# Row sums in 64 columns, spread factors by token halves, and three moved casts in a two-layer hybrid block

## The chip, the cores and the metric

The kernel runs on one core of a Trainium2 chip. The metric is device time in microseconds (us) of one execution; lower is better. Three timed runs of the kernel before gave 1850.76 us in the median (1850.59 to 1853.43).

## What is computed

The reference is a two-layer transformer block for one sequence of 256 tokens plus 256 context tokens, width 2048, everything in float32:

```
for layer i in (0, 1):
    shift, scale, gate = split(silu(c) @ ada_w[i] + ada_b[i])         # for x; the same with c_ctx for the context
    h  = rmsnorm(x,  norm_g[i]) * (1 + scale)   + shift
    hc = rmsnorm(xc, norm_g[i]) * (1 + scale_c) + shift_c
    layer 0: u, z = split(h @ w_in);  f = real(fft2(u by 16 groups of 256)) mixed by w_mix;  y = f * silu(z)   (x and xc)
    layer 1: q, k, v, z = split(h @ w_in);  rope on q and k;  attention with a sink over a window of 128 and the context;  y = o * silu(z)   (x alone)
    x  = x  + gate   * (y  @ w_out[i])
    xc = xc + gate_c * (yc @ w_out[i])                                # layer 0 alone
return rmsnorm(x, final_g)
```

`rmsnorm` divides each token's row by the root of its mean square. Layer 1 therefore needs, for each of 512 tokens, a sum over all 2048 features of layer 0's result before it can begin.

## The kernel before, in words

**Number format.** Products run on TensorE (PE) in a reduced float32 format. Each operand is split into a high part `h` (a cast, L61, on ScalarE, ACT) and a low part `l = x - h` (L62, on VectorE, DVE), and each product is three matmuls: h·h, h·l, l·h (`mm3`, L74 to L76). `half_split` (L64) splits one half (1024 columns) of a 1 MB weight tile from the pool `raw` into two tiles of the pool `ws` (6 tiles, so three pairs).

**Stages.** Stage 1 (0 to about 150 us) normalises x, makes its Fourier transform over tokens (`dft`, L238), makes layer 0's scale and shift from 32 loads of 1 MB (`ada`, L271; its matmuls are L276, four to a load), and makes the first six 128-row blocks of the gate `z` (`z_load`, `z_w`, `z_x`, `z_step`, L299 to L338). The 16 steps `k` over the features come in four rounds of four (`for i in range(4)`, L418): a round needs the scale and shift of its own features, so four `ada` loads with `which` = 1 and four with `which` = 0 for round i+1 stand among the steps of round i, with the two gate weight tiles of round i+1 (`wa` for four blocks, `wb` for two). All of these loads go through SyncE's queue (SP) in one order, into five 1 MB buffers: three of the pool `raw`, two of `raw2` (`raw_st`, L173). A load can be issued only when the instruction that last read its buffer is done: four `ada` matmuls on PE, or the splits of a gate weight tile on DVE.

Stage 2 (to about 450 us) goes through 16 Fourier groups, stage 3 makes the rest of the gate, and stage 4 (to 1018.5 us) multiplies with `w_out` of layer 0. Each of its 16 feature blocks leaves PSUM through `evac0` (L702), which also squares it (L710, ACT) and adds the squares up in `sqs[0]` (L714, L720) or leaves them in `sqs[1]`.

**The boundary of the layers** is what the change mostly touches. `x1_turn` (L758) transposes four blocks of layer 0's result into one PSUM bank (four matmuls against the identity, L761), copies it out on ACT (L763) and sends it to DRAM (L764), for two halves of the tokens and four column blocks `c`, eight times in all; `turns` (L766) queues such a pair behind named instructions. The kernel before does `c` = 0 and 1, then the row sums, then `c` = 2 and 3. A row sum (L790) is a matmul with a matrix of ones as the stationary operand and 256 columns of squares as the moving one, so every one of 128 partitions gets the sums of 256 tokens. `root` (L81) makes 1/sqrt of it on that whole 128x256 tile: a square root on ACT (L82), then on DVE a scaled copy (L83), a reciprocal (L86) and three more operations (L87 to L89). It runs twice, for x and for the context. Then, per feature block `k`, `ht` = x · scale · factor (L827, DVE), its shifted high part (L828, ACT) and its low part (L829, DVE) make the operands `hx` and `hc` of the key and value product: 16 steps of 24 matmuls on 8 PSUM banks (L74 to L76, in the loop that begins at L835). [...]

**The first keys.** After that product the keys are rotated and transposed (L866, L868), and `prep_kk` (L902) casts each key head twice into `kkh` (L908, ACT) and makes `kkl` (L910, GpSimd, POOL). The heads 0 and 1 are prepared while the query product begins.

**What sets the order.** A scheduler in the framework orders each engine's instructions when the program is built, from a model of their times; `tc.issue_after(i)` keeps instructions of a block behind `i` on `i`'s engine. The order on each engine is then fixed. Pools hand out buffers, and the reader of a buffer must be done before its next load.

Of the kernel before, what the change touches and what calls it, by code (L numbers as in the profile page):

```python
# [16 lines left out]
P = 128  # L17
# [12 lines left out]
def tile_dit(ctx: ExitStack, tc: tile.TileContext, a: dict, out: bass.AP):  # L30
# [33 lines left out]
    def half_split(t, i):  # L64
        h = wsp.tile([P, 1024], F32R, tag="ws", name="wh")
        l = wsp.tile([P, 1024], F32R, tag="ws", name="wl")
        split(h, l, t[:, i * 1024 : (i + 1) * 1024])
        return h, l

    def ws_split(t):  # L70
# [93 lines left out]
    with tc.tile_pool(name="st", reuse_waits="tile", bufs=1, side="right") as st, ExitStack() as sts:  # L164
# [22 lines left out]
        def ext(dt=F32):  # L187
            return extp[0].tile([P, 512], dt, tag="ext", name="ext")
# [115 lines left out]
        def z_w(i, wa, wb):  # L304
            pa = [half_split(wa, j) for j in range(2)]
            pb = []
            for b in range(NE - 4):
                h, l = ext(F32R), ext(F32R)
                split(h, l, wb[:, b * 512 : (b + 1) * 512])
                pb.append((h, l))  # L310
            for j in range(4):
                zw[4 * i + j] = [
                    *(tuple(t[:, (j % 2) * 512 + b * P : (j % 2) * 512 + (b + 1) * P] for t in pa[j // 2]) for b in range(4)),
                    *(tuple(t[:, j * P : (j + 1) * P] for t in p) for p in pb),
                ]
# [4 lines left out]
        def z_x(k):  # L320
            h, l = ext(F32R), ext(F32R)
            for s in range(2):
# [84 lines left out]
        ada(1, 1, 1)  # L407
        wr = z_load(0)
        dft(1, 2)
        dft(1, 3)  # L410
        sta.close()
# [4 lines left out]
        cl = ub.tile([P, 4, P], F32R, name="cl")  # L416
        z_w(0, *wr)
        for i in range(4):  # L418
            k = 4 * i
            for j in range(4):  # L420
                z_x(k + j)
            hx_prep(k)
# [335 lines left out]
    def x1_turn(tb, c):  # L758
        o = psum()
        for j in range(4):  # L760
            p_end[0] = PE.transpose(o[:, j * P : (j + 1) * P], x1[c * 4 + j][:, tb * P : (tb + 1) * P], ident).ins  # L761
        t = act()
        S.copy(t, o)  # L763
        nc.scalar.dma_start(x1d[tb, :, c * 512 : (c + 1) * 512], t)  # L764

    def turns(c, *after):  # L766
        with ExitStack() as es:
            for i in after:
                es.enter_context(tc.issue_after(i))
            for tb in range(2):  # L770
                x1_turn(tb, c)

    p_end = [None]
    o = psum()
# [5 lines left out]
    for c in range(2):  # L780
        turns(c, sq_end[0], p_end[0])
    with tc.issue_after(add_end[0]):
        V.tensor_tensor(kv_l, kv_raw[:, 0:1024], kv_h.bitcast(F32), op=ALU.subtract)
    r_bc1, qv, qt = act(), act(), act()
    for s in range(2):
        q = slice(s * N, (s + 1) * N)
        o = psum()[:, 0:N]
        with tc.issue_after(p_end[0]):
            for i in (1, 0):
                last = PE.matmul(o, ones[:, 0:1].broadcast_to([P, P]), sqs[i][:, q], start=i == 1, stop=i == 0).ins  # L790
        p_end[0] = last
        rooted = root(r_bc1[:, q], qv[:, q], qt[:, q], o)[0]
    for c in range(2, 4):
        turns(c, p_end[0], rooted)
    lay0.close()
# [19 lines left out]
    with tc.tile_pool(name="h1", reuse_waits="tile", bufs=16) as h1p:  # L815
# [3 lines left out]
        with tc.tile_pool(name="kvp", reuse_waits="tile", bufs=2) as kvp:  # L819
            hc1 = []  # L820
            for k in range(KT):
# [3 lines left out]
                for s, h in ((0, hx), (1, hc)):  # L825
                    q = slice(s * N, (s + 1) * N)
                    V.scalar_tensor_tensor(t[:, q], x1[k][:, q], gs1[:, k, s : s + 1], r_bc1[:, q], op0=ALU.mult, op1=ALU.mult)  # L827
                    S.activation(h[:, 0:N], t[:, q], AF.Identity, bias=sh1[:, k, s : s + 1])  # L828
                    hx_end = V.scalar_tensor_tensor(h[:, N : 2 * N], t[:, q], sh1[:, k, s : s + 1], h[:, 0:N].bitcast(F32), op0=ALU.add, op1=ALU.subtract).ins  # L829
                if k == 0:  # L830
                    hx_first = hx_end
                hx1.append(hx)
                hc1.append(hc)
            o = [[psum() for _ in range(2)] for _ in range(4)]
            for kg in range(8):  # L835
                w = [(kv_h, kv_l)] if kg == 0 else ws_split(raw(a["wkv"][kg]))
                for j in range(2):
                    k = kg * 2 + j
                    if k == 1:
                        with tc.issue_after(hx_first):  # L840
                            w.append(half_split(kv_raw, 1))
# [33 lines left out]
        with tc.tile_pool(name="at", reuse_waits="tile", bufs=2) as at:  # L875

            kk, qq, obs, szs = {}, {}, {}, {}
            defer = []
# [16 lines left out]
            def o1_step(k, os_, wh, wl):  # L895
                while len(yh) <= min(k + 2, NB - 1) and (len(yh) < 20 or fin):
                    y_split(len(yh))
# [4 lines left out]
            def prep_kk(hk):  # L902
                kkh = at.tile([P, 512], F32R, tag="kkh", name="kkh")
                kkl = at.tile([P, 512], F32R, tag="kkl", name="kkl")
                b = (hk % 2) * 64
                src = kT[hk // 2][b : b + 64, :]
                for c in (0, 64):
                    S.copy(kkh[c : c + 64, :], src)  # L908
                for c in (0, 64):
                    GP.tensor_tensor(kkl[c : c + 64, :], src, kkh[b : b + 64, :].bitcast(F32), op=ALU.subtract)  # L910
                kk[hk] = (kkh, kkl)
# [66 lines left out]
            def emit_unit():  # L978
# [5 lines left out]
                if pos[0] + 1 < len(ulist):  # L984
                    ready[pos[0] + 1] = prep(ulist[pos[0] + 1])
                w = ready.pop(pos[0])
                pos[0] += 1
                kind, n, i, o = u
# [349 lines left out]
```

## Time and profile before

| what | value |
|---|---|
| median of three timed runs | 1850.76 us |
| the profiled execution's own time | 1852.08 us |
| its span, first to last instruction | 1850.3 us |
| matmuls busy (PE) | 1817.7 us, 98% |
| DVE, ACT, POOL busy | 1418.7, 984.6, 154.6 us |
| DMA, mean over the span | 196 GB/s |
| DMA between 94 and 101 us | 428 GB/s |
| granted TensorE clock, 1030 to 1036 us | 0.50 |
| granted TensorE clock over the span, mean | 0.997 |

The profiled execution took 1852.08 us, of which 1850.3 us lie between its first and last instruction. PE is the busiest engine by far, so what counts is where PE stands still: the view of waits says who ended each such wait, and the view of the chain of waits follows the end of the kernel back through them. A window gives the busy time of each engine, the clock granted to TensorE (1.00 is full) and the share and rate of DMA in one stretch. In the timeline each row has a start, a length, the engine, the line, the operation, output<-inputs, and in brackets the idle time ahead of it.

### The profile page before, as it was taken

The page shows a single profiled execution, that of the slowest core. Times are in us where ns is not written, and L with a number is a line of the kernel's source. Part 1 is how long each engine was busy: PE and PEld are TensorE (multiplying, and loading weights), DVE is VectorE, ACT ScalarE, POOL GpSimd, SP SyncE. Part 2 cuts the span into 40 slices and gives each one's busy share as a digit, 9 for nine tenths or more (in the row PEclk, how much of TensorE's full clock was granted, in tenths as well). Part 3 has the DMA queues.
Part 4 walks back from the last instruction along what each step waited for, and adds up shares of the span by engine and source line. Part 5 has one row for each costly group of instructions (what it writes and reads, how often), then busy time and mean ns, then how long its engine had stood idle before and what let it go on. Part 6 is the DMA issues. An engine that isn't in the chain of part 4 may idle for free.

```text
span 1850.3 us, 26316 instructions
## 1 busy us (share of the span) xinstructions
PE 1817.7 (98%) x9933; PEld 1550.2 (84%) x9933; DVE 1418.7 (77%) x2429; ACT 984.6 (53%) x1733; POOL 154.6 (8%) x178
## 2 busy tenths in 40 slices
PE   8999999999999999999999899999999999999998
PEld 6669999988888888888888787888888888887886
DVE  5668999969788897579964926878878878887455
ACT  6545444543322242314322514888888888897343
POOL 0001000010000000000000001121220220300001
PEclk9999999999999999999999999999999999999999
DMA  9985665476676667664674333333333333434553
GB/s 364 336 337 196 214 208 188 168 267 261 259 278 252 238 220 268 238 231 153 231 280 168 115 110 140 121 131 137 115 121 131 137 117 134 160 137 175 189 182 137
DMA packets 64223, 362.75 MB, mean 196 GB/s; under 512 B 7776, under 2 KB 7920, under 8 KB 30048
## 3 DMA queue, kind: packets, MB, share of 16 engines
q1 hardware_dynamic: 52592, 326.41, 48.7%
q0 software_dynamic: 7472, 27.71, 3.9%
q10 hardware_dynamic: 4032, 6.95, 1.1%
q8 instruction: 78, 1.28, 0.3%
q14 instruction: 49, 0.40, 0.1%
HBM read 346.87 MB, written 14.16 MB: 195 GB/s over the span
## 4 chain that ended last, share of the span: by engine, by line
PE 93%; DVE 2%; ACT 2%; DMA 1%; issue 1%; POOL 0%; SPq 0%; ACTq 0%; DVEq 0%; POOLq 0%
PE ps L74 24%; PE ps L75 24%; PE ps L76 24%; PE ps L1014 6%; PE ps L1016 3%; PE ps L1070 3%; PE ps L1085 2%; PE ps L1084 2%; PE ps L1050 2%; PE ps L1051 2%; PE ps L276 1%; DVE wl L62 1%; DMA raw<-in_awp 0%; ACT wh L61 0%; DMA act<-in_xT 0%
## 5 line engine op out<-in xcount | busy, mean ns | idle before, releaser
L61 ACT CAST wh<-raw 128x1024 fp32r<-128x1024 f32 x328 | 344.1, 1053 | 449.0 <-PE ps L75 326.2
L62 DVE TENSOR_TENSOR wl<-raw,wh 128x1024 fp32r<-128x1024 f32 x328 | 414.5, 1267 | 201.2 <-ACT wh L61 198.5
L75 PE MATMUL ps<-act,wh 128*128 128x512 f32 x928 | 361.1, 389 | 0.0
L74 PE MATMUL ps<-act,wh 128*128 128x512 f32 x928 | 357.6, 389 | 0.0
L76 PE MATMUL ps<-act,wl 128*128 128x512 f32 x928 | 356.3, 389 | 0.0
L75 PEld LDWEIGHTS ps<-act,wh 128*128 128x128 f32 x928 | 174.2, 188 | 36.4 <-DVE act L641 0.2
L76 PEld LDWEIGHTS ps<-act,wl 128*128 128x128 f32 x928 | 174.2, 188 | 36.3 <-DVE wl L62 0.2
L74 PEld LDWEIGHTS ps<-act,wh 128*128 128x128 f32 x928 | 174.1, 188 | 36.2 <-ACT act L640 0.3
L1014 PE MATMUL ps<-h,wh 128*128 128x512 f32 x512 | 186.8, 400 | 0.0
L611 DVE CUSTOM_DVE_ANT_0 raw<-raw,cb 128x1024 f32<-128x1024 f32 x128 | 155.0, 1221 | 35.1 <-DMA raw<-in_adw 34.1
L611 DVE CUSTOM_DVE_ANT_0 junk<-raw,cb 128x1024 f32<-128x1024 f32 x96 | 117.2, 1221 | 32.7 <-DMA raw<-in_adw 19.0
L1016 PE MATMUL ps<-h,wl 128*128 128x256 f32 x512 | 138.1, 280 | 0.0
L74 PE MATMUL ps<-wh,h 128*128 128x512 f32 x320 | 125.1, 399 | 6.3 <-ACT h L828 6.3
L75 PE MATMUL ps<-wl,h 128*128 128x512 f32 x320 | 126.5, 395 | 1.5 <-DVE wl L62 1.5
L76 PE MATMUL ps<-wh,h 128*128 128x512 f32 x320 | 124.4, 391 | 0.0
L1014 PEld LDWEIGHTS ps<-h,wh 128*128 128x128 f32 x512 | 96.1, 188 | 18.7
L1052 DVE CUSTOM_DVE_ANT_0 ps<-ps,mask,nsink 128x512 f32<-128x512 f32 x128 | 92.1, 754 | 11.8 <-PE ps L1051 10.6
L1055 ACT ACTIVATE p<-ps,mx 128x512 f32<-128x512 f32 x128 | 87.3, 687 | 24.6 <-DVE mx L1052 24.0
L1016 PEld LDWEIGHTS ps<-h,wl 128*128 128x128 f32 x512 | 96.8, 189 | 1.4
L62 DVE TENSOR_TENSOR pl<-ps,ph 128x512 fp32r<-128x512 f32 x128 | 83.7, 685 | 10.0 <-ACT ph L61 8.9
L1060 ACT ACTIVATE p<-p,sm 128x512 f32<-128x512 f32 x128 | 85.5, 718 | 7.8 <-DVE sm L1058 7.8
L75 PE MATMUL ps<-wl,ys 128*128 128x512 f32 (+1 forms) x216 | 84.0, 389 | 0.0
(328 smaller groups left out, 3790.5 us busy)
## 6 DMA issues: line engine op xcount, KB each, us to landing
raw<-in_adw SPq DMA_DIRECT2D x64, 1024.0 KB, 5.3
raw<-in_wz SPq DMA_DIRECT2D x62, 1024.0 KB, 4.9
raw<-in_awp SPq DMA_DIRECT2D x32, 1024.0 KB, 7.8
raw<-in_wo SPq DMA_DIRECT2D x32, 1024.0 KB, 5.7
raw<-in_wq SPq DMA_DIRECT2D x32, 1024.0 KB, 4.8
raw<-in_wu SPq DMA_DIRECT2D x25, 1016.0 KB, 5.5
raw<-in_wo1b SPq DMA_DIRECT2D x16, 1024.0 KB, 4.8
act<-in_xT POOLq DMA_DIRECT2D x32, 256.0 KB, 5.8
```

The source lines that it names most:

```text
L61: S.copy(h, src)
L62: V.tensor_tensor(l, src, h.bitcast(F32), op=ALU.subtract)
L74: PE.matmul(o, wh, xh, start=start, stop=False)
L75: PE.matmul(o, wh, xl, start=False, stop=False)
L76: PE.matmul(o, wl, xh, start=False, stop=stop)
L611: V.tensor_tensor_reduce(junk if s == 0 and i < 3 else wf, wf, cb[:, s], 1.0, 0.0, ALU.mult, ALU.add, acc[:, i, kh, fg * 2 + f, s : s + 1])
L1014: PE.matmul(o[0], wh[:, q], hx1[k], start=k == 0, stop=k == KT - 1)
L1016: PE.matmul(o[0][:, 0:N], wl[:, q], hx1[k][:, 0:N], start=False, stop=False)
L1052: V.tensor_tensor_reduce(o, o, mask[:, tb, :], -0.125, nsink[:, i : i + 1], ALU.add, ALU.min, mx[:, tb : tb + 1])
L1055: S.activation(pt[:, tb, :], so[tb], AF.Exp, bias=mx[:, tb : tb + 1], scale=-1.0, accum_out=sm[:, tb : tb + 1])
L1060: S.activation(pt[:, tb, :], pt[:, tb, :], AF.Copy, scale=sm[:, tb : tb + 1])
L1070: PE.transpose(o[:, (kt * 2 + tb) * P : (kt * 2 + tb + 1) * P], pt[:, tb, c : c + P], ident)
```

## The change

In stage 1, `half_split` keeps its last cast in `cast[0]`. The gate weights of round 0 are split (`z_w(0)`) ahead of the last two transforms, with `wb` split as one half into `ws` tiles in place of four `ext` tiles, and the operand of step 0 (`z_x(0)`) is made ahead of the last transform, in `act` tiles.

At the boundary, the turns of `c` = 0 and 1 only transpose at first; `x1_out` copies and sends later. The row sums use the squares as the stationary operand and 64 columns of ones as the moving one, four token blocks in turn, so that a sum lies on its token's partition. `root` runs once, on one column of each block (128x4). The turns of `c` = 2 follow, then two matmuls for each token half spread the factors over all partitions (as `bcast_rows` does, L98), ACT copies each half out, and the first `ht` (k = 0) reads it from PSUM. The turns of `c` = 3 follow; four of the eight copies out wait for the first shifted high parts (`hx_act`).

In the attention stage, the casts of the keys 0 and 1 wait for the weight cast of the fourth unit (`kk_hold`); `kkl` of head 0 is made on DVE. In the last product, layer 1's results are split up to six steps ahead (two before) while `k` < 12.

```diff
--- before
+++ after
@@ -64,8 +64,11 @@
     def half_split(t, i):
         h = wsp.tile([P, 1024], F32R, tag="ws", name="wh")
         l = wsp.tile([P, 1024], F32R, tag="ws", name="wl")
-        split(h, l, t[:, i * 1024 : (i + 1) * 1024])
+        cast[0] = S.copy(h, t[:, i * 1024 : (i + 1) * 1024]).ins
+        V.tensor_tensor(l, t[:, i * 1024 : (i + 1) * 1024], h.bitcast(F32), op=ALU.subtract)
         return h, l
+
+    cast = [None]
 
     def ws_split(t):
         return [half_split(t, i) for i in range(2)]
@@ -305,8 +308,13 @@
             pa = [half_split(wa, j) for j in range(2)]
             pb = []
             for b in range(NE - 4):
-                h, l = ext(F32R), ext(F32R)
-                split(h, l, wb[:, b * 512 : (b + 1) * 512])
+                if i == 0:
+                    if b == 0:
+                        h0, l0 = half_split(wb, 0)
+                    h, l = (t[:, b * 512 : (b + 1) * 512] for t in (h0, l0))
+                else:
+                    h, l = ext(F32R), ext(F32R)
+                    split(h, l, wb[:, b * 512 : (b + 1) * 512])
                 pb.append((h, l))
             for j in range(4):
                 zw[4 * i + j] = [
@@ -318,7 +326,7 @@
         z_l = {}
 
         def z_x(k):
-            h, l = ext(F32R), ext(F32R)
+            h, l = (ext(F32R), ext(F32R)) if k else (act(F32R), act(F32R))
             for s in range(2):
                 q = slice(s * N, (s + 1) * N)
                 t = xT[k // 2][s][:, (k % 2) * N : (k % 2 + 1) * N]
@@ -405,8 +413,9 @@
         turn(0, 0, rows)
         ada(1, 1, 0)
         ada(1, 1, 1)
-        wr = z_load(0)
+        z_w(0, *z_load(0))
         dft(1, 2)
+        z_x(0)
         dft(1, 3)
         sta.close()
         wfp = us.enter_context(tc.tile_pool(name="wfp", reuse_waits="tile", bufs=8))
@@ -414,11 +423,11 @@
         ub = us.enter_context(tc.tile_pool(name="ub", reuse_waits="tile", bufs=1))
         ch = ub.tile([P, 4, P], F32R, name="ch")
         cl = ub.tile([P, 4, P], F32R, name="cl")
-        z_w(0, *wr)
         for i in range(4):
             k = 4 * i
             for j in range(4):
-                z_x(k + j)
+                if k + j:
+                    z_x(k + j)
             hx_prep(k)
             if 0 < i < 3:
                 ada(i + 1, 1, 0)
@@ -759,18 +768,14 @@
         o = psum()
         for j in range(4):
             p_end[0] = PE.transpose(o[:, j * P : (j + 1) * P], x1[c * 4 + j][:, tb * P : (tb + 1) * P], ident).ins
+        turned.append((tb, c, o))
+
+    def x1_out(tb, c, o):
         t = act()
         S.copy(t, o)
         nc.scalar.dma_start(x1d[tb, :, c * 512 : (c + 1) * 512], t)
 
-    def turns(c, *after):
-        with ExitStack() as es:
-            for i in after:
-                es.enter_context(tc.issue_after(i))
-            for tb in range(2):
-                x1_turn(tb, c)
-
-    p_end = [None]
+    p_end, turned = [None], []
     o = psum()
     p_end[0] = PE.transpose(o[0:KT, 0:P], gt1.rearrange("p k s -> p (k s)"), ident).ins
     gr = const.tile([KT, P], F32, name="gr")
@@ -778,20 +783,40 @@
         S.copy(gr, o[0:KT, 0:P])
     nc.gpsimd.dma_start(gated.rearrange("o (k p) -> (o k) p", p=P), gr)
     for c in range(2):
-        turns(c, sq_end[0], p_end[0])
+        with tc.issue_after(p_end[0]):
+            for tb in range(2):
+                x1_turn(tb, c)
+    with tc.issue_after(sq_end[0]):
+        for _ in range(2):
+            x1_out(*turned.pop(0))
+    o = psum()
+    for i in (1, 0):
+        for t in range(4):
+            with tc.issue_after(p_end[0]):
+                p_end[0] = PE.matmul(o[:, t * 64 : (t + 1) * 64], sqs[i][:, t * P : (t + 1) * P], ones[:, 0:1].broadcast_to([P, 64]), start=i == 1 and t == 0, stop=i == 0 and t == 3).ins
+    qr, qv, qt = (const.tile([P, 4], F32, name=f"q{n}") for n in "rvt")
     with tc.issue_after(add_end[0]):
-        V.tensor_tensor(kv_l, kv_raw[:, 0:1024], kv_h.bitcast(F32), op=ALU.subtract)
-    r_bc1, qv, qt = act(), act(), act()
+        add_end[0] = V.tensor_tensor(kv_l, kv_raw[:, 0:1024], kv_h.bitcast(F32), op=ALU.subtract).ins
+    with tc.issue_after(add_end[0]):
+        rooted, q_end = root(qr, qv, qt, o.rearrange("p (t c) -> p t c", c=64)[:, 0:4, 0])
+    with tc.issue_after(rooted):
+        for _ in range(2):
+            x1_out(*turned.pop(0))
+    with tc.issue_after(p_end[0]):
+        for tb in range(2):
+            x1_turn(tb, 2)
+    r_bc1 = act()
+    rows1 = []
     for s in range(2):
-        q = slice(s * N, (s + 1) * N)
         o = psum()[:, 0:N]
-        with tc.issue_after(p_end[0]):
-            for i in (1, 0):
-                last = PE.matmul(o, ones[:, 0:1].broadcast_to([P, P]), sqs[i][:, q], start=i == 1, stop=i == 0).ins
-        p_end[0] = last
-        rooted = root(r_bc1[:, q], qv[:, q], qt[:, q], o)[0]
-    for c in range(2, 4):
-        turns(c, p_end[0], rooted)
+        for t in range(2):
+            with tc.issue_after(p_end[0]):
+                p_end[0] = PE.matmul(o[:, t * P : (t + 1) * P], qr[:, 2 * s + t : 2 * s + t + 1].broadcast_to([P, P]), ident, start=True, stop=True).ins
+        spread = S.copy(r_bc1[:, s * N : (s + 1) * N], o).ins
+        rows1.append(o)
+    with tc.issue_after(p_end[0]):
+        for tb in range(2):
+            x1_turn(tb, 3)
     lay0.close()
 
     l1c = ctx.enter_context(tc.tile_pool(name="l1c", reuse_waits="tile", bufs=1))
@@ -824,11 +849,14 @@
                 t = kvp.tile([P, 512], F32, tag="ht", name="ht")
                 for s, h in ((0, hx), (1, hc)):
                     q = slice(s * N, (s + 1) * N)
-                    V.scalar_tensor_tensor(t[:, q], x1[k][:, q], gs1[:, k, s : s + 1], r_bc1[:, q], op0=ALU.mult, op1=ALU.mult)
-                    S.activation(h[:, 0:N], t[:, q], AF.Identity, bias=sh1[:, k, s : s + 1])
+                    V.scalar_tensor_tensor(t[:, q], x1[k][:, q], gs1[:, k, s : s + 1], r_bc1[:, q] if k else rows1[s], op0=ALU.mult, op1=ALU.mult)
+                    hx_act = S.activation(h[:, 0:N], t[:, q], AF.Identity, bias=sh1[:, k, s : s + 1]).ins
                     hx_end = V.scalar_tensor_tensor(h[:, N : 2 * N], t[:, q], sh1[:, k, s : s + 1], h[:, 0:N].bitcast(F32), op0=ALU.add, op1=ALU.subtract).ins
                 if k == 0:
-                    hx_first = hx_end
+                    hx_first = (hx_end, hx_act)
+                    with tc.issue_after(hx_act):
+                        while turned:
+                            x1_out(*turned.pop(0))
                 hx1.append(hx)
                 hc1.append(hc)
             o = [[psum() for _ in range(2)] for _ in range(4)]
@@ -837,7 +865,7 @@
                 for j in range(2):
                     k = kg * 2 + j
                     if k == 1:
-                        with tc.issue_after(hx_first):
+                        with tc.issue_after(hx_first[0]), tc.issue_after(hx_first[1]):
                             w.append(half_split(kv_raw, 1))
                     wh, wl = w[j]
                     for tb in range(4):
@@ -874,6 +902,7 @@
         oA, curw, kg1, yh = [], [None], [0], []
         with tc.tile_pool(name="at", reuse_waits="tile", bufs=2) as at:
 
+            kk_hold = []
             kk, qq, obs, szs = {}, {}, {}, {}
             defer = []
 
@@ -893,7 +922,7 @@
                 yh.append(t)
 
             def o1_step(k, os_, wh, wl):
-                while len(yh) <= min(k + 2, NB - 1) and (len(yh) < 20 or fin):
+                while len(yh) <= min(k + (6 if k < 12 else 2), NB - 1) and (len(yh) < 20 or fin):
                     y_split(len(yh))
                 for tb in range(2):
                     mm3(os_[tb], yh[k][:, tb * P : (tb + 1) * P], yh[k][:, N + tb * P : N + (tb + 1) * P], wh, wl, k == 0, k == NB - 1)
@@ -904,10 +933,11 @@
                 kkl = at.tile([P, 512], F32R, tag="kkl", name="kkl")
                 b = (hk % 2) * 64
                 src = kT[hk // 2][b : b + 64, :]
+                with tc.issue_after(kk_hold[0]) if hk < 2 else nullcontext():
+                    for c in (0, 64):
+                        S.copy(kkh[c : c + 64, :], src)
                 for c in (0, 64):
-                    S.copy(kkh[c : c + 64, :], src)
-                for c in (0, 64):
-                    GP.tensor_tensor(kkl[c : c + 64, :], src, kkh[b : b + 64, :].bitcast(F32), op=ALU.subtract)
+                    (GP if hk else V).tensor_tensor(kkl[c : c + 64, :], src, kkh[b : b + 64, :].bitcast(F32), op=ALU.subtract)
                 kk[hk] = (kkh, kkl)
 
             def finish_q(hk, oq):
@@ -984,6 +1014,8 @@
                 if pos[0] + 1 < len(ulist):
                     ready[pos[0] + 1] = prep(ulist[pos[0] + 1])
                 w = ready.pop(pos[0])
+                if pos[0] == 3:
+                    kk_hold.append(cast[0])
                 pos[0] += 1
                 kind, n, i, o = u
                 if kind == "o":
```

## The prediction

> **What bounds the kernel now.** I read the page first: the busy times, then the shares of the chain that ended last.
>
> ```profile
> span 1850.3 us, 26316 instructions
> ...
> PE 1817.7 (98%) x9933; PEld 1550.2 (84%) x9933; DVE 1418.7 (77%) x2429; ACT 984.6 (53%) x1733; POOL 154.6 (8%) x178
> ...
> PE 93%; DVE 2%; ACT 2%; DMA 1%; issue 1%; POOL 0%; SPq 0%; ACTq 0%; DVEq 0%; POOLq 0%
> ```
>
> PE holds the end: 1817.7 of 1850.3 us busy. The change removes almost no PE work, so it can only win where PE stands still or runs at a low clock. The view of PE's waits lists those places:
>
> ```profile
> PE ps L257 <- DMA xn<-in_x: 6.4, 1, 6.4
> PE ps L74 <- ACT h L828: 6.3, 1, 6.3
> PE ps L74 <- ACT ext L326: 2.3, 1, 2.3
> PE ps L276 <- DMA raw<-in_awp: 1.8, 1, 1.8
> PE ps L75 <- DVE wl L62: 1.5, 1, 1.5
> ```
>
> The first is the start and isn't touched. The second is the boundary of the layers, the third and fourth lie in stage 1, the fifth is the first keys: each part of the change has its own wait, 11.9 us in all. The sum is made against the profiled execution (1852.08 us, 1850.3 of them span); the median of the runs is 1.32 us less.
>
> **The boundary.** The timeline of before:
>
> ```profile
> 1018.48 1.91 PE L761 MATMUL ps<-ident,act 128*128 128x128 f32 x16
> ...
> 1019.36 1.48 DVE L720 TENSOR_TENSOR act<-act 128x512 f32<-128x512 f32 x2
> ...
> 1020.16 1.05 ACT L763 COPY act<-ps 128x512 f32<-128x512 f32 x2
> ...
> 1020.22 2.23 PE L790 MATMUL ps<-act,ones 128*128 128x256 f32 x8
> ...
> 1020.75 1.22 DVE L783 TENSOR_TENSOR wl<-raw,wh 128x1024 fp32r<-128x1024 f32 x1
> ...
> 1021.59 1.04 ACT L61 CAST wh<-raw 128x1024 fp32r<-128x1024 f32 x1
> ...
> 1023.85 1.74 DVE L86 RECIPROCAL act<-act 128x256 f32<-128x256 f32 x1
> ...
> 1025.79 1.74 DVE L86 RECIPROCAL act<-act 128x256 f32<-128x256 f32 x1
> ...
> 1029.39 1.67 DVE L827 SCALAR_TENSOR_TENSOR ht<-act,gs 128x256 f32<-128x256 f32 x4
> 1029.91 0.91 ACT L828 ACTIVATE h<-ht,sh 128x256 fp32r<-128x256 f32 x2 [4.17 <-DVE ht L827]
> 1030.46 0.79 PE L74 MATMUL ps<-wh,h 128*128 128x512 f32 x1 [6.26 <-ACT h L828]
> ```
>
> PE's sums start at 1020.22 and end at 1022.45; the roots hold DVE until 1029.39, almost all of it in work on 256 columns; two reciprocals alone take 3.48. The small root of the start, the spreading matmuls (four of them are the eight records) and a 256-column copy out of PSUM give the new prices:
>
> ```profile
> 11.44 0.30 ACT L82 ACTIVATE rt<-s,epsd 128x2 f32<-128x2 f32 x1 [0.23 <-DVE s L216]
> ...
> 12.12 0.16 DVE L86 RECIPROCAL rr<-rt 128x2 f32<-128x2 f32 x1
> 12.31 0.16 DVE L87 TENSOR_TENSOR rt<-rr 128x2 f32<-128x2 f32 x1
> ...
> 34.34 1.06 PE L101 MATMUL ps<-ident,rr 128*128 128x128 f32 x8
> ...
> 1123.82 0.38 ACT L61 CAST act<-ps 128x256 fp32r<-128x256 f32 x1
> ```
>
> Step by step, in the order of instructions of the built program. Transposes of c = 0, 1 and the adds of L720 stay, so the sums start at 1020.22 again. They are eight matmuls in sixteen records with 128 rows to load each; at the transposes' cadence (1.91 / 16 = 0.12) they end at 1022.15. No row has a matmul of 64 columns with squares as the stationary operand: none could be under half the cadence (1021.2), none over the 0.28 of a sum's record (2.23 / 8; 1024.7); the load of 128 rows is what a transpose has too, so 0.12. The square root of 128x4 by the 128x2 row 0.30 plus a hand-over: 1022.55. L83 and L86 to L89 are five steps of 0.195 (12.12 to 12.31): 1023.55. Eight transposes of c = 2 (0.95) run beside. Two spreading matmuls for a half 0.5: 1024.15. The copy 0.38, which L827 is queued behind: 1024.6 with the hand-over. From L827 to L828 0.52 and from there to PE 0.55 (1029.39, 1029.91, 1030.46): first product at about **1025.7** (1025.0 to 1026.8), where before had 1030.46: gain 4.8 (3.7 to 5.5).
>
> The wl of L783 (1.22) ends before the root needs DVE. After the start, ACT still has four copies (0.52 each) and the cast of the second weight half (1.04) ahead of step 1; with the wl of 1.22 behind it this half is ready about 1031. In the built order PE uses it after 32 matmuls of 0.222, 7.1 us after 1025.7. The banks that the four copies free are wanted from the 13th matmul on, 1028.4, and the copies end one by one from 1027.4 on. Hidden, with 1 to 2 us over; its failure is a rival.
>
> The clock is the second term:
>
> ```profile
> 1029.00:1030.00 1.00, 0.00 (x0) 0.00 (x0) 1.00 (x4) 0.09 (x1) 0.00 (x0) 0.70 0.00 0
> 1030.00:1036.00 6.00, 5.54 (x13) 4.37 (x14) 6.00 (x12) 3.46 (x7) 0.00 (x0) 0.50 0.24 63
> 1036.00:1042.00 6.00, 6.00 (x27) 4.90 (x27) 6.00 (x15) 3.68 (x7) 0.00 (x0) 0.98 0.27 113
> ```
>
> The last number but two is the granted clock. It fell in the last microsecond of the wait and stayed at 0.50 for 13 matmuls, 5.54 / 13 = 0.426 each, where 27 took 6.00, 0.222: 13 x 0.204 = 2.65. The wait of 2.3 at 54.87 lowered nothing. In the new order the longest stand is about 0.5 and no stretch without an ordinary matmul is over 2 us, so I count **2.7** as gained. Boundary: 7.5.
>
> [...]
>
> **The first keys.**
>
> ```profile
> 1126.93 2.54 ACT L908 CAST kkh<-act 64x512 fp32r<-64x512 f32 x4
> ...
> 1129.49 2.94 ACT L61 CAST wh<-raw 128x1024 fp32r<-128x1024 f32 x3
> ...
> 1130.58 4.38 DVE L62 TENSOR_TENSOR wl<-raw,wh 128x1024 fp32r<-128x1024 f32 x2 [5.00 <-ACT wh L61]
> ...
> 1132.79 0.50 PE L75 MATMUL ps<-wl,h 128*128 128x512 f32 x1 [1.46 <-DVE wl L62]
> ```
>
> Four key casts hold ACT for 2.54 ahead of the weight cast. Behind that cast instead, the cast runs at 1127.0, and wl ends about 1129.4 (1.04 and 1.22), ahead of its use at 1131.3. The keys are used after the query product. Gain **1.46**; if the later weight casts then wait for the keys' casts, 0.5 is left.
>
> **Stage 1.** Here I expect a loss.
>
> ```profile
> 50.34 2.00 ACT L61 CAST wh<-raw 128x1024 fp32r<-128x1024 f32 x2
> ```
>
> ```profile
> 79.78 1.00 PE ps L276 x8
> ...
> 84.41 0.99 PE ps L276 x8
> ...
> 97.38 3.57 PE ps L276 x32
> ```
>
> ```profile
> 127.53 1.07 PE ps L276 x8
> ```
>
> ```profile
> 85.47 7.34 SPq L182 DMA_DIRECT2D raw<-in_awp  x4
> ```
>
> ```profile
> 72.50 2.04 SPq L182 DMA_DIRECT2D raw<-in_awp  x3
> ...
> 75.07 0.33 SPq L182 DMA_DIRECT2D raw<-in_wz  x1
> ```
>
> ```profile
> raw<-in_wz SPq DMA_DIRECT2D x1, 1024.0 KB, 11.2
> ```
>
> These are the timeline, the chain of waits, SP's timeline and the time to landing of the load issued at 75.07. The split weights of round 0 and the operand of step 0 are made by 54 (the casts ran from 50.34 on anyway), so the wait of 2.33 at 54.87 goes. But in the built order the `ada` groups move against the gate's matmuls. Before, the second group of round 1 (84.41) stands 15 matmuls behind the first (79.78), and the third and fourth follow after 9 and 9 more. After, it stands 43 behind, with the third and fourth directly on it; and the next four groups (97.38) follow only 11 matmuls later (before 21). The first group ends about 78.5 (80.78 less 2.3); 43 x 0.225 = 9.7 and 1.0 give 89.2 for the second, 90.2, 91.2 for the others. SP's issue at 85.47 comes 0.07 after the second group's end at 85.40: the loads of `which` = 0 wait for these buffers. So its four loads are issued from 89.3 to 91.2 (before 85.47 to 92.81), and PE wants them at 94.25. A burst of four lands late: issued from 72.50 to 75.07, the last landed at 86.3, 11.2 after its issue. So the last of the new burst lands about 102.4 (101.8 to 103.2), and its matmuls and the next end at 104.4, where before had 100.95. From there before needed 27.65 to the end of its last `ada` group (127.53 and 1.07), of them the wait of 1.8; so after ends it at 104.4 + 25.85 = 130.2 against 128.6: a loss of **1.6**. The 1.8 goes, as the loads meet a later PE. Bounds: no stall at all gives the gain of 2.3, with the other wait too 4.1; if the last load lands 3 us later still, a loss of 4.6.
>
> **The rest.** Splits up to six steps ahead change one pair in the built order: 0, with 0.4 either way by the waits of L1084 and L1085 it could touch. The two `kkl` of head 0 on DVE are used only after the query product.
>
> Sum: 7.5 + 1.46 - 1.6 = 7.4; 1852.08 becomes 1844.7, and at the median 1850.76 **1843.4**, say 1843.5.
>
> **The rivals.**
> 1. *The loads keep up* in stage 1 (the burst meets a freer queue): plus 2.3 in place of minus 1.6 is 3.9 more, 1839.5; 1837.7 if the wait of 1.8 goes too. For: the first loads of the burst of 72.50 landed much sooner than its last one. Against: the landing row above.
> 2. *The clock falls in the boundary anyway*: 2.7 back, 1846.2.
> 3. *ACT holds up step 1*: four copies (2.1) and the cast (1.04) ahead of the second weight half come after PE has run out, all 3.1 exposed: 1846.6. For: the margins above are 1 to 2 us, and ACT also issues the copies' DMAs in between. Against: each copy frees its own bank.
> 4. *Slower*: the late release of the `ada` buffers comes again in each of three rounds, in place of once. Without a stall the group of round 1 would end at 97.8 (94.25 and 3.57), so its stall is 6.6, and the forecast holds it once; twice more is 13.2: 1843.4 + 13.2 = 1856.6. It decides where a round's loads are issued less than some 9 us ahead of their last use. For: round 2 has the same order of calls. Against: only round 1 has the shift of 28 matmuls in the built order.
> 5. *The boundary doesn't move*: the adds (L720 and L783) or the copies set the start of `ht`, and only the keys gain, against the 1.6: 1850.9.
>
> **How the numbers follow.** Forecast 0.50, rivals 0.17, 0.09, 0.09, 0.09 and 0.06. The forecast's own range is 1840.4 (stage 1 without loss or gain, boundary at 1025.0) to 1847.6 (boundary at 1026.8, stage 1 at its worst bound). A range of 1838.5 to 1849 holds it with rivals 1 to 3 and leaves out 4, 5 and the lower end of 1, below 0.2. A measurement here can tell about 0.2% (3.7 us) from no change: faster is below 1847.06, slower above 1854.46. Faster: the forecast but 0.03 of it, rival 1, and most of 2 and 3, with some of their spread on the other side: 0.76; same 0.15; slower 0.09.
>
> **What would show it.** The boundary: PE's stand after the last transposes about 0.5, first key product about 7 us after the first transposes, clock 1.00 over these 7 us and the 6 that follow. Keys: the wait of L75 for wl near 1131 gone. Stage 1: a wait of L276 for a DMA of 5 to 7 us around 95 to 103, SP's issues of the loads ahead of it at 89 to 92, and no wait for L326. Wrong would be: a clock of 0.50 at the first key product, a PE wait for wl at step 1, no stall near 95, or one in each round.

## The result and the profile after

The changed kernel took 1845.61 us in the median of nine runs (1844.76 to 1847.6); nine runs of the kernel before beside it had 1851.59 (1849.39 to 1855.25). The ratio is 0.9968, with a 95% interval from 0.9957 to 0.9978: 6.0 us faster (4.1 to 8.0). The forecast was 1843.5, 7.3 us faster; the measured time lies in the stated range, and the direction was right.

Line numbers shift: after the change L77 to L79 are the three product matmuls (before L74 to L76), L279 the scale matmuls (L276), L68 a weight's low part (L62), L770 the turns (L761), L796 the row sums (L790), L85 to L92 the root, L852 and L853 the first operands (L827, L828).

The page of the changed kernel, its busy times:

```profile
span 1843.9 us, 26342 instructions
...
PE 1817.1 (99%) x9949; PEld 1548.7 (84%) x9949; DVE 1415.4 (77%) x2425; ACT 985.3 (53%) x1733; POOL 152.1 (8%) x176
```

PE is busy for as long as before (1817.7); the span is 6.4 us shorter. PE's waits:

```profile
PE ps L260 <- DMA xn<-in_x: 6.1, 1, 6.1
PE ps L279 <- DMA raw<-in_awp: 5.2, 2, 3.9
PE ps L77 <- ACT dh L225: 1.9, 1, 1.9
PE ps L1116 <- ACT ph L61: 1.1, 2, 0.7
PE ps L79 <- DVE wl L68: 1.1, 2, 0.8
PE ps L77 <- ACT ys L61: 0.8, 1, 0.8
PE ps L814 <- ACT act L775: 0.4, 1, 0.4
...
PE ps L77 <- ACT h L853: 0.2, 1, 0.2
```

The boundary's 6.3, the 2.3 for `ext` and the 1.5 for a low part are gone. In place of 1.8 for a scale load there are 5.2. Two waits of the kernel before at the start of stage 2 are gone as well, which the prediction did not name:

```profile
PE ps L75 <- DVE ml L62: 1.1, 1, 1.1
PE ps L75 <- DVE apl L62: 0.9, 1, 0.9
```

The boundary in the timeline:

```profile
1021.33 1.91 PE L770 MATMUL ps<-ident,act 128*128 128x128 f32 x16
...
1023.07 1.94 PE L796 MATMUL ps<-ones,act 128*128 128x64 f32 x16
...
1025.05 0.26 ACT L85 ACTIVATE qt<-ps,epsd 128x4 f32<-128x4 f32 x1 [0.99 <-PE ps L796]
...
1026.02 0.16 DVE L92 SCALAR_TENSOR_TENSOR qr<-qt,qr 128x4 f32<-128x4 f32 x1
...
1026.33 1.13 PE L814 MATMUL ps<-ident,qr 128*128 128x128 f32 x8 [0.44 <-ACT act L775]
1027.05 0.82 ACT L815 COPY act<-ps 128x256 f32<-128x256 f32 x2 [0.77 <-PE ps L814]
...
1027.45 0.48 DVE L852 SCALAR_TENSOR_TENSOR ht<-act,gs,ps 128x256 f32<-128x256 f32 x1 [1.27 <-ACT act L815]
...
1028.53 0.50 PE L77 MATMUL ps<-wh,h 128*128 128x512 f32 x1 [0.20 <-ACT h L853]
```

From the first transpose to the first key product it is 1028.53 - 1021.33 = 7.20 us (before 1030.46 - 1018.48 = 11.98): 4.78 gained. The clock over this stretch, by windows (the last number but two):

```profile
1021.00:1028.00 7.00, 6.56 (x58) 6.20 (x57) 4.65 (x13) 4.37 (x11) 0.51 (x1) 1.00 0.40 150
1028.00:1030.00 2.00, 1.80 (x9) 1.33 (x8) 2.00 (x6) 2.00 (x5) 0.00 (x0) 1.00 0.02 6
1030.00:1036.00 6.00, 6.00 (x28) 4.96 (x27) 5.00 (x10) 6.00 (x11) 0.00 (x0) 1.00 0.69 249
```

It stays at 1.00. In stage 1, the chain of waits, PE's timeline and two windows show what was lost:

```profile
91.66 10.53 DMA raw<-in_awp
102.23 3.42 PE ps L279 x16
```

```profile
94.87 1.07 PE L279 MATMUL ps<-raw,c 128*32 128x512 f32 x8
97.26 1.06 PE L279 MATMUL ps<-raw,c 128*32 128x512 f32 x8 [1.33 <-DMA raw<-in_awp]
102.23 3.42 PE L279 MATMUL ps<-raw,c 128*32 128x512 f32 x16 [3.91 <-DMA raw<-in_awp]
...
128.98 2.78 PE L279 MATMUL ps<-raw,c 128*32 128x512 f32 x24
```

```profile
98.32:102.23 3.91, 0.01 (x1) 0.00 (x0) 1.15 (x3) 0.00 (x0) 0.00 (x0) 0.96 1.01 427
102.23:105.58 3.35, 3.35 (x16) 0.59 (x16) 0.00 (x0) 0.00 (x0) 0.00 (x0) 0.54 1.02 428
```

```profile
89.91 2.78 SPq L185 DMA_DIRECT2D raw<-in_awp  x5
```

The last row is SP's timeline: the loads that were issued from 85.47 on now go from 89.91, in one burst, and the one issued about 91.66 takes 10.53 us. PE stands 3.91 us at its matmuls and then runs them at a clock of 0.54: 16 records in 3.42 us, where before 32 took 3.64. The last scale matmul ends at 131.76 (before 128.60): 3.2 us late.

### The profile page after: what moved, and what is told of

It reads as the page before. It is cut to its first block, busy times and chain, and to the rows that moved or that the text cites. A ratio compares the mean times of both kernels' runs of the same rounds, so it can differ in the third digit from the quotient of the medians.

```text
span 1843.9 us, 26342 instructions
## 1 busy us (share of the span) xinstructions
PE 1817.1 (99%) x9949; PEld 1548.7 (84%) x9949; DVE 1415.4 (77%) x2425; ACT 985.3 (53%) x1733; POOL 152.1 (8%) x176
## 4 chain that ended last, share of the span: by engine, by line
PE 93%; DMA 2%; issue 2%; DVE 1%; ACT 1%; SPq 0%; POOL 0%; ACTq 0%; POOLq 0%; DVEq 0%
PE ps L77 24%; PE ps L79 24%; PE ps L78 24%; PE ps L1046 6%; PE ps L1048 3%; PE ps L1102 3%; PE ps L1117 2%; PE ps L279 2%; PE ps L1116 2%; PE ps L1082 2%; PE ps L1083 2%; DMA raw<-in_awp 1%; DMA raw<-in_adw 1%; DMA cb<-in_crow 1%; DVE junk L620 0%
## 5 line engine op out<-in xcount | busy, mean ns | idle before, releaser
L68 DVE TENSOR_TENSOR wl<-raw,wh 128x1024 fp32r<-128x1024 f32 x329 | 415.5, 1266 | 190.3 <-ACT wh L67 186.3
L77 PE MATMUL ps<-act,wh 128*128 128x512 f32 x934 | 360.0, 389 | 0.0
L79 PE MATMUL ps<-act,wl 128*128 128x512 f32 x934 | 358.5, 389 | 1.1 <-DVE wl L68 1.1
L79 PEld LDWEIGHTS ps<-act,wl 128*128 128x128 f32 x934 | 175.3, 188 | 38.3 <-DVE wl L68 2.2
L77 PEld LDWEIGHTS ps<-act,wh 128*128 128x128 f32 x934 | 175.2, 188 | 36.3 <-ACT act L649 0.2
L79 PE MATMUL ps<-wh,h 128*128 128x512 f32 x320 | 124.5, 391 | 0.0
L77 PE MATMUL ps<-wh,h 128*128 128x512 f32 x320 | 123.1, 396 | 0.2 <-ACT h L853 0.2
L62 DVE TENSOR_TENSOR pl<-ps,ph 128x512 fp32r<-128x512 f32 x128 | 83.7, 685 | 9.9 <-ACT ph L61 8.7
```

What stands on the lines that cost most here:

```text
L62: V.tensor_tensor(l, src, h.bitcast(F32), op=ALU.subtract)
L68: V.tensor_tensor(l, t[:, i * 1024 : (i + 1) * 1024], h.bitcast(F32), op=ALU.subtract)
L77: PE.matmul(o, wh, xh, start=start, stop=False)
L79: PE.matmul(o, wl, xh, start=False, stop=stop)
```

## The experiments

My theory: four gains and losses that add up, boundary 4.8, clock 2.65, first keys 1.46, stage 1 a loss by loads that are issued late because their buffers come free late. The rivals are named with each run. Every ratio is to runs of the kernel before on the same chip. The medians of those runs lay between 1851.4 and 1852.9, so the medians of two rows compare no better than to some 1.5 us.

| kernel | median, us | ratio (95% interval) | span, us |
|---|---|---|---|
| the change | 1845.61 | 0.9968 (0.9957 to 0.9978) | 1843.9 |
| no_stage1 | 1844.99 | 0.9962 (0.9949 to 0.9974) | 1841.2 |
| stage1_only | 1854.62 | 1.0014 (1.0005 to 1.0023) | 1852.9 |
| pinned | 1839.80 | 0.9935 (0.9923 to 0.9948) | 1837.3 |
| zx_late | 1846.55 | 0.9962 (0.9951 to 0.9974) | 1844.9 |
| boundary_only | 1846.43 | 0.9967 (0.9957 to 0.9978) | 1846.3 |
| wide_root | 1851.14 | 0.9998 (0.9989 to 1.0007) | 1850.1 |
| fill_mm | 1850.01 | 0.9989 (0.9980 to 0.9998) | 1845.7 |
| fill_tp | 1849.00 | 0.9985 (0.9976 to 0.9993) | 1844.9 |
| fill_short | 1853.26 | 1.0000 (0.9989 to 1.0011) | 1851.1 |
| keys_only | 1849.51, one run | | 1847.7 |
| ahead_two | 1845.10 | 0.9964 (0.9951 to 0.9976) | 1843.0 |
| no_ysplit (spoilt) | 1980.84 | 1.0686 (1.0666 to 1.0707) | 1979.9 |

**Stage 1 alone and left out.** `stage1_only` has the first three hunks of the diff and those of the loops that call `z_w` and `z_x`; `no_stage1` has all but these, and keeps the first hunk, which the keys' edit needs.

> Only the stage 1 part of the change. My theory, that four scale and shift loads are issued late because their buffers come free late: about 3 us slower than before, with the loads issued at 90 to 91.7, a PE wait for a load of 4 to 5.5 us between 95 and 102 and a granted clock of 0.50 just after it; by 132 PE is 3.2 us late. Rival, that this wait has its cause in another part or that the clock alone costs: no wait there, 0 to 2.3 us faster than before.

Measured: 2.6 us slower (0.9 to 4.3). The loads are issued from 90.23 on, PE's timeline has the wait as in the whole change, the clock over 100 to 110 us is 0.66, and the last scale matmul ends at 132.66, 4.1 us later than before (128.60):

```profile
102.53 3.64 PE L279 MATMUL ps<-raw,c 128*32 128x512 f32 x16 [3.86 <-DMA raw<-in_awp]
```

> The change without its stage 1 part: gate weights of round 0 are split after the last transforms, as before. My theory, that the parts add up and stage 1 alone loses: 4.8 (start of the key product) + 2.7 (clock) + 1.5 (first keys) = 9.0 us faster than the kernel before, 3 us faster than the whole change, and PE waits 2.3 us at 54.9 again. Rival, that the stage 1 part gains as such and the boundary costs what is missing: slower than the whole change, 4 to 6 us faster than before.

Measured: 7.0 us faster than before (4.8 to 9.4), 9.1 by the span, with the wait of 2.32 for `ext` at 54.5 again. The interval holds my 9.0 and the rival's 6 alike; by the medians it is 0.6 us faster than the whole change, by the spans 2.7. This run does not decide; that stage 1 loses rests on the run above, the next, and the traces: the last scale matmul ended between 126.5 and 131.1 in the seven kernels with the old stage 1, and between 131.6 and 134.2 in the five that split these weights early and hold nothing.

**The order held.** In `pinned` the gate matmuls of round 1 may not pass the scale matmuls:

```diff
+            if i == 1:
+                e1 = ada_end[0]
+                z_step(k, range(5))
...
+                e2 = ada_end[0]
...
+                with tc.issue_after(e1):
+                    z_step(k, [5])
+                    z_step(k + 1, [0, 1])
+                with tc.issue_after(e2):
+                    z_step(k + 1, [2, 3, 4])
+                with tc.issue_after(ada_end[0]):
+                    z_step(k + 1, [5])
```

> The whole change, with the gate matmuls of round 1 held behind the scale loads' matmuls: the second group stands 15 matmuls behind the first (43 in the change), the next two directly on it, the following four 35 later (11). Nothing else is altered. My theory, late release: the loads are issued at 83 to 86 in place of 90 to 91.7, the wait near 95 to 102 falls from 5.2 to at most 1.5, the clock stays at 1.00, and the kernel is 4 to 5.5 us faster than the change. Rival, that the transfers themselves are the limit (the rate is 427 GB/s there): the loads land hardly sooner, a wait of over 3.5 us stays, within 1 us of the change.

Measured: 5.8 us below the change, a little over the 5.5 expected, and 12.0 below the kernel before (9.6 to 14.3). PE's and SP's timelines, and two windows:

```profile
84.00 2.78 PE L279 MATMUL ps<-raw,c 128*32 128x512 f32 x24 [1.64 <-DMA raw<-in_awp]
95.47 1.06 PE L279 MATMUL ps<-raw,c 128*32 128x512 f32 x8
97.59 2.78 PE L279 MATMUL ps<-raw,c 128*32 128x512 f32 x24
```

```profile
85.13 14.77 SPq L185 DMA_DIRECT2D raw<-in_awp  x8
```

```profile
84.00:106.00 22.00, 22.00 (x129) 12.93 (x129) 12.25 (x36) 7.56 (x15) 0.56 (x1) 1.00 0.98 395
94.00:106.00 12.00, 12.00 (x73) 6.29 (x71) 6.54 (x21) 3.92 (x9) 0.56 (x1) 1.00 1.01 413
```

The second, third and fourth groups run together at 84.0, the loads behind them go out from 85.13, and PE never stands from 84 to 106 us. The bytes are the same and the rate is 413 GB/s against 427, so it was the time of issue and not the transfers' speed. No wait is left near 95 to 102. One of 1.64 is new, ahead of 84.0, for the second group's own load. This kernel beats both.

**Which edit moves the order.** `zx_late` makes the operand of step 0 after the last transform again, and leaves the early split of the weights.

> The whole change, but the operand of step 0 is made after the last transform, as before; the gate weights of round 0 are still split early. In the built order the second scale group of round 1 again stands 43 gate matmuls behind the first. My theory: the early split of the weights makes the late release, so the loads are again issued at about 90 to 92, with a PE wait for a load of 3.5 to 5.5 us between 95 and 104 and a clock of 0.50 behind it. Rival, that the early operand of step 0 (PE runs ahead by 2.3 us) makes it: the wait is 2.3 us shorter or more, and the clock holds.

Measured: waits of 1.32 and 3.92 at 97.0 and 99.4, issues from 91.00 on, clock 0.50 from 102 to 106. So the early split of the weights is enough for the late order. It also takes most of the wait of 2.3 for `ext`, of which 0.48 is left without the early operand:

```profile
55.47 1.67 PE L77 MATMUL ps<-ext,wh 128*128 128x512 f32 x6 [0.48 <-ACT ext L334]
```

What the early operand does alone was not run.

**The boundary alone, and the wide root in the new order.** `boundary_only` has the boundary's hunks alone. `wide_root` is the whole change with two sums of 256 columns and two roots as before, and no spreading:

```diff
-    for i in (1, 0):
-        for t in range(4):
...
+    for s in range(2):
+        o = psum()[:, 0:N]
...
+            q = slice(s * N, (s + 1) * N)
+            rooted = root(r_bc1[:, q], qv[:, q], qt[:, q], sums[s])[0]
```

> Only the boundary part. My theory: 7.2 us from the first transpose to the first key product (before 11.98), clock 1.00, PE's longest stand there 0.45; 4.8 + 2.65 = 7.4 us faster than before, with the waits of stage 1 and of the first keys as in the kernel before. Rival, that half of it is given back later (the copies moved behind the first products free banks late): 3 to 5 us faster, with new PE waits between 1030 and 1060.

Measured: 1028.92 - 1021.72 = 7.20 us, clock 1.00, no new wait up to 1060; 6.1 us faster (4.1 to 8.0), which holds the 7.4. The rival's 3 to 5 lies partly in it too, but the new waits that it needs are not there.

> The whole change, but the row sums as wide as before (128 stationary ones, 256 columns) and the root on two 128x256 tiles, without spreading; the new order of turns and copies stays. Before has 11.98 us from the first transpose to the first key product, the change 7.20. My theory, that the width of the root on DVE holds the start: 10.4 to 11.5 us here, and the kernel 3.5 to 7 us slower than the change (the clock falls or not). Rival, that ACT's copies ahead of the square root held it and the new order alone brings the gain: 7.2 to 8.5 us, within 1.5 us of the change.

Measured: 1033.03 - 1022.41 = 10.62 us, and 5.5 us slower than the change. From its timeline:

```profile
1025.57 0.47 ACT L85 ACTIVATE act<-ps,epsd 128x256 f32<-128x256 f32 x1 [0.42 <-PE ps L798]
...
1026.41 1.74 DVE L89 RECIPROCAL act<-act 128x256 f32<-128x256 f32 x1
...
1028.35 1.74 DVE L89 RECIPROCAL act<-act 128x256 f32<-128x256 f32 x1
...
1031.95 1.66 DVE L848 SCALAR_TENSOR_TENSOR ht<-act,gs 128x256 f32<-128x256 f32 x4
1032.47 0.91 ACT L849 ACTIVATE h<-ht,sh 128x256 fp32r<-128x256 f32 x2 [4.60 <-DVE ht L848]
1033.03 0.80 PE L77 MATMUL ps<-wh,h 128*128 128x512 f32 x1 [4.89 <-ACT h L849]
```

Of the 4.78, the new order of copies brings 1.36 (11.98 - 10.62) and the narrow root with its narrow sums 3.42 (10.62 - 7.20). The prediction named only the root as what holds the start; its steps needed both, as its square root also started without the copies ahead of it. The 5.5 is more than the 3.42, as the clock is low again behind the stand of 4.89 (0.50 over 1033 to 1036).

**The clock by itself.** The kernel before, with matmuls (`fill_mm`) or transposes (`fill_tp`) on data at hand in the idle stretch; their results are not used.

```diff
+    o = psum()
+    for _ in range(26):
+        with tc.issue_after(p_end[0]):
+            p_end[0] = PE.matmul(o, kv_h[:, 0:P], kv_h[:, 0:512], start=True, stop=True).ins
```

> The kernel before, with 26 matmuls of 128x512 on data at hand (their result is not used) put into PE's idle time at the boundary, between the last transposes and the first key product. They take 26 x 0.222 = 5.8 us of the 6.26 and nothing waits for them. My theory, that the idle time costs a second time because the clock falls: the first key product starts at the same time after the first transpose (11.98 us), the granted clock stays 1.00, the 13 products at 0.426 us become 0.222 and the kernel is 2.65 us faster. Rival, that the slow products have another cause (their operands come late): clock 1.00 but no gain, the products still 0.4 us apart.

> The same place filled with 48 transposes of 128x128 in place of matmuls (96 records of 0.119 us by the cadence of before, 5.7 us; result not used). If transposes hold the clock as matmuls do, as the trace of before suggests: clock 1.00 in the first products, 2.65 us faster, like the other filling. If transposes do not count as activity: the clock falls about 5 us after 1022.3, where the last row sum ended, the transposes themselves slow to 0.2 us, the first product comes later than 11.98 us after the first transpose or starts at clock 0.50, and the gain is 0 or a loss of up to 3 us.

Measured: in both the first product comes 11.99 us after the first transpose, the clock is 1.00 and 28 products run in the 6 us from 1030 on; 2.0 us faster (0.4 to 3.7) and 2.8 (1.3 to 4.4), both in keeping with 2.65. PE in `fill_tp`:

```profile
1021.44 5.40 PE L798 MATMUL ps<-ident,act 128*128 128x128 f32 x48
1027.86 0.50 PE L74 MATMUL ps<-wh,h 128*128 128x512 f32 x1 [1.02 <-ACT h L832]
1028.43 0.39 PE L74 MATMUL ps<-wh,h 128*128 128x512 f32 x1
```

Behind the transposes the clock was 1.00, as behind the matmuls. The 48 took 5.40 us; the cadence of before (1.91 / 16 = 0.119 us a record) gives 5.7 for the 48 records that the profile shows, where the expectation had 96.

> The kernel before, with 12 filling matmuls (2.7 us) in place of 26 in the idle time at the boundary, so that about 3.5 us of it are left. The clock has held in every stand of 2.3 us but one and fell in the stands of 3.9 and 6.3 us seen so far. If the length of one stand decides and 3.5 us is enough: clock 0.50 at the first key product, the gain of the long filling (2.65) gone, within 0.5 us of the kernel before. If it takes 4 us or more: clock 1.00, 2.65 us faster.

Measured: no gain (1.0000, and the interval leaves out 2.65 us). PE stood from 1029.03 to 1032.53, and single microseconds show the clock:

```profile
1031.00:1032.00 1.00, 0.00 (x0) 0.00 (x0) 1.00 (x4) 0.03 (x1) 0.00 (x0) 1.00 0.00 0
1032.00:1033.00 1.00, 0.47 (x2) 0.43 (x3) 1.00 (x3) 1.00 (x3) 0.00 (x0) 0.99 0.00 0
1033.00:1034.00 1.00, 1.00 (x4) 0.75 (x3) 1.00 (x4) 1.00 (x3) 0.00 (x0) 0.50 0.00 0
```

A stand of 3.50 us was enough here, and the clock fell only after PE had begun again at 1032.53 (0.99 over 1032 to 1033, 0.50 over the next): the fall lay not within the stand but behind it.

**The small parts.**

> Only the later casts of the first keys and the low part of head 0 on DVE. My theory: the wait of 1.46 us for a weight's low part near 1131 goes and nothing takes its place, 1.46 us faster (below what one run can tell, so by the trace). Rival: the casts held back delay the next weight casts, and a wait of 0.5 us or more comes in the next 10 us.

Measured: the wait near 1131 is gone and no other of 0.5 us or more comes near it; the one run shows no time.

> The whole change with layer 1's results split two steps ahead, as before. I took this edit as worth nothing: within 0.4 us of the change by the trace (the last 170 us of the span as long as in the change). Rival: it is what shortens the end, and the span from the wait near 1166 on is 1 us or more longer.

This kernel was spoilt: by a mistake of mine it also made every weight's low part twice, and says nothing of the splits. With DVE busy for 1784.3 us in place of 1415.4, it was 135 us longer than the change.

> The whole change with layer 1's results split two steps ahead, as before, and nothing else altered (the run before this one made every weight's low part twice by mistake). I took this edit as worth nothing: the span from PE's wait for ph near 1166 to the end is within 0.4 us of the change's 677.2, and the time within 1.5 us of the change. Rival, that it is what shortens the end: 1 us or more longer there.

Measured: 1843.0 - 1165.80 = 677.2 us from PE's wait for `ph` to the end, as in the change (1843.9 - 1166.68 = 677.2); 1845.1 us. The edit is worth nothing here.

## Why the prediction held, and where it was off

- **What bounds the kernel**: right. PE's busy time moved by 0.6 us, its waits and its clock made the result.
- **The boundary**: right step by step, counted from the first transpose. Sums ended after 3.68 us (forecast 3.67), the square root after 3.98 (4.07), the root after 4.85 (5.07), `ht` began after 6.12 (6.1), the first product after 7.20 (7.2). The 0.12 for a 64-column matmul's record held: 1.94 for 16. The stand of 0.5 came in two pieces, 0.44 ahead of the spreading, by the row for a copy out of PSUM (L775), and 0.20 ahead of the product. The root's lead of 0.22 on its forecast was used up there.
- **The clock**: right (1.00 in each window from 1021 to 1036), and shown by itself by the two fillings (2.0 and 2.8 us faster, forecast 2.65). Rival 2 is out. That the clock needs ordinary matmuls, for which the prediction's "no stretch without an ordinary matmul" allows, no run shows: behind the 5.40 us of transposes in `fill_tp`, which the rows list as MATMUL against `ident`, it was 1.00.
- **The first keys**: right by the traces, the wait of 1.46 went and nothing took its place; no run weighs it by time.
- **Copies that run PE dry** (rival 3) and **a boundary that doesn't move** (rival 5): not seen; there is no PE wait between 1028.5 and 1060.
- **Stage 1**: the mechanism was right (issues from 89.91, forecast 89.3; last landing at 102.2, forecast 102.4; shown by `pinned`), and the size was off. I priced the loss at 1.6 at the end of the last scale matmul; it was 3.2 (131.76 against 128.60). The term that failed is the stalled group's end, "its matmuls and the next end at 104.4": it was 105.6. The waits were shorter than my 6.6 (1.33 and 3.91), but I left out what I had counted at the boundary, the low clock behind a stand: behind the 3.91 us it was 0.54, and 16 records took 3.42 us where 1.82 would do (half of the 3.64 for 32 before), 1.6 more (I had put 2.0 for them, and the load landed 0.2 earlier). From there to the last scale matmul it took 26.1, where I had put 25.85.
- **The rest**: "0, with 0.4 either way" was too narrow for stage 2 and 3. Two waits of before (1.07 and 0.94, at 168 and 176) went. They stand in all seven profiles with the old stage 1 and in none of the six with the early split, not even in `pinned`, where PE comes earlier than before; so they belong to the edit of stage 1, by a path that I did not trace. Two small waits (0.77 at 438.7, 0.34 at 803.9) and some 0.6 us of PE time between 180 and 1020 came. By trace: 3.2 - 2.0 + 1.7 (stage 1 to the boundary, 1021.33 - 1018.48 = 2.85) - 4.78 - 2.65 - 1.46 = -6.0; the other 0.4 of the span's 6.4 lie behind the first key product, in pieces that I did not follow. That the sum of 7.4 came so near to this is luck in part: the 1.6 too little in stage 1 and the 1.7 after it stand against 2.0 that I had not seen.
- **The lower end of the forecast's own range** was summed up wrongly: 5.46 (boundary at 1025.0), 2.7 and 1.46 with no loss give 9.6 and so 1841.1, not 1840.4. The stated range was wider and is not touched by it.
- **Rival 4** (a stall in each round) did not come: in the change the other rounds had no wait for a load at all. `pinned` shows a gain like rival 1's once the loads are issued in time: its last scale matmul ends 1.6 us before that of the kernel before (127.02 against 128.60; rival 1 had 2.3), and the boundary is reached 3.7 us before (1014.68 against 1018.37, first matmul of the gate row), 2.0 of it by the two waits that went.

What stays open: how much of the spread from run to run lies in stage 1. Five kernels with the same stage 1 (before, boundary_only, fill_mm, fill_tp, fill_short) reached the boundary at 1018.4, 1021.6, 1016.5, 1015.8 and 1020.4, so one profile cannot weigh an edit there to better than some 6 us, and the 3.2 above is that of two profiles; the runs of `stage1_only` (0.9 to 4.3 slower) hold it and the 1.6 alike. The stretch at the boundary repeated to 0.01 us.

## What to carry to other kernels

A stall is to be priced twice: the wait itself, and the low clock behind it (here 0.50 behind PE's stands of 3.5 us in `fill_short`, 3.9 in the change, 4.9 in `wide_root` and 6.3 in the kernel before, and behind some of 2.3); I did it in one stage and forgot it in another. When work is made ready earlier, read the new order of the engine that consumes it: weights that are split early can let other matmuls pass the ones that free a load's buffer, and the loss shows at the next use of that buffer. A few lines that held those matmuls back turned 6.0 us of gain into 12.0.

## What the runs showed of the hardware that I had not expected

The length of one stand did not settle the clock. The wait of 2.3 us in stage 1 left it at 1.00 in the profiles of before, no_stage1, keys_only, fill_mm and fill_tp, and lowered it in boundary_only and fill_short, to 0.50. From boundary_only, with PE standing from 54.89 to 57.21:

```profile
57.00:58.00 1.00, 0.79 (x3) 0.65 (x4) 1.00 (x4) 1.00 (x4) 0.00 (x0) 0.82 1.21 303
58.00:59.00 1.00, 1.00 (x4) 0.82 (x3) 1.00 (x5) 1.00 (x3) 0.00 (x0) 0.50 0.82 336
59.00:60.00 1.00, 1.00 (x4) 0.72 (x3) 1.00 (x5) 1.00 (x4) 0.00 (x0) 0.50 1.25 377
60.00:61.00 1.00, 1.00 (x4) 0.81 (x3) 1.00 (x5) 0.80 (x3) 0.00 (x0) 0.50 0.66 279
61.00:62.00 1.00, 1.00 (x6) 0.83 (x5) 1.00 (x5) 1.00 (x3) 0.00 (x0) 0.97 1.06 451
```

By the 0.82 the fall comes some 0.4 us after the work has begun again, and by the 0.97 it ends some 3.4 us later. The matmuls follow each other at 0.43 us there (59.57, 60.00, 60.42), in place of 0.23 in the kernel before, and PE reaches the same matmul 4.90 us after the wait (62.11 - 57.21) in place of 3.32 (60.52 - 57.20): a loss of 1.6 us. What decides whether a stand of 2.3 us pays it was not isolated; before, boundary_only and fill_short have the same stage 1.

Nor had the same stand one price. Behind the wait of 3.9 us in stage 1 the clock was at 0.50 for 3.4 us in the change and for 6.8 in `stage1_only`:

```profile
101.90:105.30 3.40, 3.07 (x16) 0.59 (x16) 0.00 (x0) 0.00 (x0) 0.00 (x0) 0.50 1.02 429
```

```profile
100.40:107.20 6.80, 4.67 (x19) 1.50 (x20) 0.00 (x0) 0.58 (x1) 0.00 (x0) 0.50 1.02 426
```

In the kernel before it was at 0.50 from 1029.4 to 1036.2, 6.8 again. So the 1.6 us that the low clock took in the change is the price of the shorter of two lengths. PE worked from 102.53 on in `stage1_only`; half of the time to 107.2, 2.3 us, is an estimate of the longer one's.
